# Pinning SyncE's loads to program order in a hybrid decoder layer, with the mLSTM's row of maxima on GpSimd's queue

## The chip, the cores and the metric

The kernel runs on one core of one Trainium2 chip. The metric is device time in microseconds of that core for one execution. TensorE (PE) multiplies, VectorE (DVE), ScalarE (ACT) and GpSimd (POOL) do element work, and SyncE (SP) only issues transfers. POOL and ACT issue transfers as well. Each engine takes its own instructions strictly in the order in which they stand in its queue: one that waits holds up all that stand behind it on the same engine.

## The reference, cut to what matters

One step of a one-layer decoder for 2048 prompt tokens and 8 x 4 decode tokens, model width 1024. An mLSTM head group (4 heads, keys of 64, values of 128) and a sliding-window attention group (8 heads, window 128, a learned sink per head) share one input and one output projection; a squared-ReLU MLP of width 4096 and a gated per-layer embedding follow.

```
def mlstm_chunk(state, blk):                       # 128 tokens
    b = cumsum(lf); log_d = where(causal, b_t - b_s + ig_s, -inf)
    m_t = maximum(b + m_prev, max(log_d))          # the row of maxima
    s = einsum('bhtd,bhsd->bhts', q, k) * exp(log_d - m_t)
    num = s @ v + exp(b + m_prev - m_t) * (q @ c_prev)
    den = sum(s) + exp(b + m_prev - m_t) * (q @ n_prev)
    h = num / maximum(abs(den), exp(-m_t))
...
x1 = x + rms_norm(concat(mlstm, attention) @ w_out, g_mix_post)
x2 = x1 + rms_norm(relu(rms_norm(x1, g_ffn_pre) @ w_up)**2 @ w_down, g_ffn_post)
y  = x2 + gated embedding of p through w_pgate and w_pproj
```

All of it is in float32; the kernel multiplies with a split of each operand into a high and a low part, three matmuls for one product.

## The kernel before, in words

The 2048 tokens are 16 blocks of 128 (numbered 0 to 15). The first part (0 to about 680 us) is the input projection over six chunks of 3, 3, 3, 3, 2 and 2 blocks; the mLSTM and the window attention of a chunk run as side work between the projection's matmuls. The second part goes over three groups of two chunks each: the output projection (`mo`), the MLP (`up`, `dn`) and the gate (`pg`, `pv`). In a group, two plain MLP steps are followed by 14 steps in which the up-projection is done with seven products instead of eight, from sums and differences of weight blocks (`product`); those are the product steps.

**Weights** go through a `Ring`. In the first use of a weight its raw float32 tile (`wr`, five buffers; `wb` for the product steps) is loaded on SP, ACT casts it to the high part, DVE or POOL subtracts to get the low part (`wsplit`), and POOL stores the pair to device memory (`wk<-w`). All later uses reload the pair (`w<-wk`, 512 KB, SP) into one of seven pair buffers. So the second and later chunks of a part only reload, and the third group never splits. A pair buffer comes free when PE has done the matmuls that read it: SP waits at the head of its queue for this.

**What sets the order.** The program is written as Python that emits instructions; the tile framework places every instruction on its engine's queue, and may move an instruction up or down among its neighbours unless it was marked with `here` (`tc.keep_in_program_order`), after which it keeps its turn among the others so marked. Matmuls, splits, and the stores of pairs are marked. The loads through `dma` (that is, `nc.sync.dma_start`) are not, and nor are those through `put` (`nc.gpsimd.dma_start`).

**The row of maxima.** `mbd` is a small array in device memory that holds the row of m_t for the blocks of one chunk; ACT stores it (`mbd<-Mt`, line 906). `weights(i)` (line 959) then loads it into `Wt`, the same row on all 128 partitions, 256 KB (line 961), on SP. DVE adds the causal mask (line 962), ACT takes exp (line 964), DVE multiplies by the scores (line 997, `Wt<-mS,Wt`). There are 16 such loads, one for each block, and two `Wt` buffers.

**Names that the prediction uses.** `wr<-in_w_out`, `in_w_up`, `in_w_down`: raw weights (lines 351, 363, 374); `wb<-in_w_up` (line 307): the raw tile of a product step, two for each step; `xr` (line 1460, POOL): the input block added after the output projection, used at line 1485; `y<-yd` (line 848): the mixers' output read back; `scs`, `snr`, `sso`: the decode tokens' states, loaded by POOL in group 2 of 3; `gffn`, `gpost`: the weights of the norms after the MLP and after the output projection (line 1453); `os` (line 831): sigmoid of the output gate; `hh`, `hl` (lines 231, 232): the split hidden activations; `x31t`: a transpose on PE.

Of the kernel before, what the change touches and what calls it, by code (L numbers as in the profile page):

```python
# [18 lines left out]
P = 128  # L19
# [103 lines left out]
def bc(ap, axis, n):  # L123
    v = ap.unsqueeze(axis)
    shape = list(v.shape)
    shape[axis] = n
    return v.broadcast_to(tuple(shape))
# [71 lines left out]
def hybrid_layer(ctx: ExitStack, tc: tile.TileContext, A, O):  # L199
    nc = tc.nc  # L200
    act, dve, pool = nc.scalar, nc.vector, nc.gpsimd
    pe = Flow(tc)
    swa, mls, tsp = pe.side(), pe.side(), pe.side()
    dma, put = nc.sync.dma_start, nc.gpsimd.dma_start
    here = tc.keep_in_program_order

    xp = A["x_prompt"].rearrange("b t d -> (b t) d")
    xs = A["x_sample"].rearrange("b t d -> (b t) d")
# [726 lines left out]
    def mlstm_finish(num, e_col, sig, y, n, nm):  # L935

        t = small.tile([P, 24], F32, tag="fin", name=nm + "f", bufs=2)
        den = num[:n, :, 128]
        dve.scalar_tensor_tensor(t[:n, 0:4], den, -1.0, den, ALU.mult, ALU.max)
        dve.scalar_tensor_tensor(t[:n, 4:8], e_col, 8.0, t[:n, 0:4], ALU.mult, ALU.max)  # L940
        dve.reciprocal(t[:n, 8:12], t[:n, 4:8])
        junk = jp.tile([P, MV], BF16, tag="jm", name=nm + "jm")
        for h in range(MH):
            act.activation(junk[:n], num[:n, h, 0:MV], AF.Square, scale=t[:n, 8 + h : 9 + h], accum_out=t[:n, 12 + h : 13 + h])
        dve.tensor_scalar(t[:n, 16:20], t[:n, 12:16], 1.0 / MV, EPS, ALU.mult, ALU.add)
        pool.tensor_tensor(t[:n, 20:24], t[:n, 16:20], nhalf[:n].broadcast_to((n, 4)), ALU.pow)
        dve.tensor_tensor(t[:n, 20:24], t[:n, 20:24], t[:n, 8:12], ALU.mult)
        for h in range(MH):
            c = slice(h * MV, (h + 1) * MV)
            dve.scalar_tensor_tensor(y[:n, c], num[:n, h, 0:MV], t[:n, 20 + h : 21 + h], sig[:n, c], ALU.mult, ALU.mult)  # L950

    def mlstm_chunk(r, blocks):
        nonlocal C
        qk, col = r["qk"], r["col"]
        rows = lambda h: slice((h % 2) * MK, (h % 2) * MK + MK)
        cq = lambda i, q, h: col[:, i * 16 + q * 4 + h : i * 16 + q * 4 + h + 1]
        Ws = {}

        def weights(i):
            Wt = sm.tile([P, MH, P], F32, tag="Wt", name=f"Wt{blocks[i]}")  # L960
            dma(Wt, bc(r["mbd"][:, i * P : (i + 1) * P], 0, P))
            here(dve.tensor_tensor(Wt, Wt, bc(mask, 1, MH), ALU.add))
            for h in range(MH):
                act.activation(Wt[:, h], Wt[:, h], AF.Exp, bias=cq(i, 0, h), scale=-1.0)
            Ws[i] = Wt

        todo = []

        def finish():
            if todo and len(r.get("o", ())) == len(blocks):  # L970
                i, num = todo.pop(0)
                y = sm.tile([P, 512], F32, tag="ym", name=f"ym{blocks[i]}")
                mlstm_finish(num, col[:, i * 16 + 8 : i * 16 + 12], r["o"][i], y, P, f"m{blocks[i]}")
                put(yd[blocks[i]][0], y)

        weights(0)
        yield 3.0
        for i, b in enumerate(blocks):
            c = slice(i * P, (i + 1) * P)
            v = r["v"][i]  # L980
            if i + 1 < len(blocks):
                weights(i + 1)
            pK = psum(ps_m, f"mK{b}")
            for p in range(2):
                pe.transpose(pK[:, p * P : (p + 1) * P], qk[2 + p][:, c], ident)
            kw = sm.tile([P, MH, MK], F32, tag="kw", name=f"kw{b}")
            dve.tensor_tensor(
                kw, pK[:, 0:256].rearrange("p (h d) -> p h d", h=MH), bc(col[:, i * 16 + 12 : i * 16 + 16], 2, MK), ALU.mult
            )
            yield MPACE  # L990
            pS = [psum(ps_m, f"mS{b}{e}")[:, : 2 * P].rearrange("p (h t) -> p h t", h=2) for e in range(2)]
            for h in range(MH):
                pe.matmul(pS[h % 2][:, h // 2], qk[2 + h // 2][rows(h), c], qk[h // 2][rows(h), c], start=True, stop=True)
            Wt = Ws.pop(i)
            We = Wt.rearrange("p (g e) t -> p e g t", e=2)
            for e in range(2):
                dve.tensor_tensor(We[:, e], pS[e], We[:, e], ALU.mult)
            while len(todo) > 1:
                finish()
                yield 0.5  # L1000
            num = sm.tile([P, MH, 130], F32, tag="num", name=f"num{b}")
            yield MPACE
            if C is not None:
                pX = [psum(ps_m, f"mX{b}{p}").rearrange("p (h t) -> p h t", h=2) for p in range(2)]
                for h in range(MH):
                    pe.matmul(pX[h % 2][:, h // 2, :130], qk[h // 2][rows(h), c], C[rows(h), h // 2], start=True, stop=True)
                for h in range(MH):
                    dve.tensor_scalar(num[:, h], pX[h % 2][:, h // 2, :130], cq(i, 1, h), None, ALU.mult)
                yield MPACE
            pI = [psum(ps_m, f"mI{b}{p}").rearrange("p (h t) -> p h t", h=2) for p in range(2)]  # L1010
            for h in range(MH):
                pe.matmul(pI[h // 2][:, h % 2, :130], Wt[:, h], v[:, h], start=True, stop=True)
            for p in range(2):
                n_ = num[:, 2 * p : 2 * p + 2]
                if C is None:
                    act.copy(n_, pI[p][:, :, :130])
                else:
                    dve.tensor_tensor(n_, pI[p][:, :, :130], n_, ALU.add)
            yield MPACE
            pU = psum(ps_m, f"mU{b}").rearrange("p (h t) -> p h t", h=2)  # L1020
            for h in range(MH):
                pe.matmul(pU[rows(h), h // 2, :130], kw[:, h], v[:, h], start=True, stop=True)
            Cn = sm.tile([P, 2, 130], F32, tag="C", name=f"C{b}")
            for p in range(2):
                if C is None:
                    dve.tensor_copy(Cn[:, p], pU[:, p, :130])
                else:
                    dve.scalar_tensor_tensor(
                        Cn[:, p], C[:, p], col[:, 64 + 4 * p + i : 65 + 4 * p + i], pU[:, p, :130], ALU.mult, ALU.add
                    )  # L1030
            C = Cn
            todo.append((i, num))
            finish()
            yield MPACE
        while todo:
            finish()
            yield 0.5
# [413 lines left out]
    def gain(src, nm):  # L1451
        g = gp.tile([P, D], F32, tag="g", name=nm)
        dma(g, src[0:1, :].broadcast_to((P, D)))
        return g

    gpost, gffn = gain(A["norm_mix_post"], "gpost0"), None
# [41 lines left out]
    f, yt, ut, xt = {}, {}, {}, {}  # L1498
# [126 lines left out]

    def mlp(gi, chunks, sample):
        nonlocal gffn
        gffn = gain(A["norm_ffn_post"], f"gffn{gi}")
        G = f"{gi}"
        if sample:  # L1630
            f["t"] = es2.enter_context(tc.tile_pool(name="ft", bufs=1, reuse_waits="tile")).tile(
# [154 lines left out]
        for ci in range(2):  # L1786
            if ci == 1:
                pe.drain(tsp)
                pe.drain(dec)
                es_lp.close()  # L1790
                es_t = ExitStack()
                tp = es_t.enter_context(tc.tile_pool(name="tp", bufs=1, side="right", reuse_waits="tile"))
                ring.wide = es_t.enter_context(tc.tile_pool(name="wide", bufs=WIDE, side="right", reuse_waits="tile"))
                tsp.add(sums())
            for s in range(FAST):
                if ci == 0:
                    hids.append({})
                up(s, ci, ring.take(4), hids[s])
            for s in range(FAST):
                for half in range(2):  # L1800
                    down(s, ci, half, down_weights(), hids[s])
# [23 lines left out]
    def finish(b, half, pg, pv, n, nm, last):  # L1825
        hs = slice(half * 512, half * 512 + 512)
        t = gw.tile([P, 512], F32, tag="sg", name=f"sg{nm}{half}")
        act.activation(t[:n], pg, AF.Tanh, scale=0.5)
        dve.scalar_tensor_tensor(t[:n], t[:n], 1.0, pv, ALU.add, ALU.mult)
        o = gw.tile([P, 512], F32, tag="ot", name=f"ot{nm}{half}")  # L1830
        dve.scalar_tensor_tensor(o[:n], t[:n], 0.5, f[b][:n, hs], ALU.mult, ALU.add)
        dst = y_s[:, hs] if b == "s" else y_p[b * P : (b + 1) * P, hs]
        (dma if last else put)(dst, o[:n])

    def gate_post(gi, ci, c, sample):

# [168 lines left out]
```

## Time and profile before

| what | value |
|---|---|
| time, median of 3 runs | 2611.8 us (2611.41 to 2611.95) |
| the profiled execution: time, span | 2623.78 us, 2621.7 us |
| mean granted TensorE clock | 0.989 |
| PE busy / idle | 2534.7 us (97%) / 87 us |
| DVE, ACT, POOL busy | 57%, 37%, 24% |
| transfers: mean rate, share of the 16 engines | 248 GB/s; SP's queue 53.4%, POOL's 17.3% |
| `w<-wk` on SP, 512 KB | 728 loads, 4.9 us from issue to landing (median) |
| `Wt<-mbd` on SP, 256 KB | 16 loads, 4.2 us |
| `xr` on POOL, 512 KB | 16 loads, 9.4 us |

PE is busy 97% of the span, so the time is PE's work plus what PE waits: the last is 87 us, spread over many short waits. The views of waits list what ended each wait; the timeline lists an engine's instructions with their start, their length and, in square brackets, the idle time just before and what ended it.

### The profile page before, as it was taken

The numbers are of one execution on the slowest core, as the hardware profiler recorded it, in microseconds if no ns is written. First come the engines' busy times: TensorE is split into PE (matmuls) and PEld (weight loads), VectorE is DVE, ScalarE is ACT, GpSimd is POOL, SyncE is SP. The second block draws the span as 40 slices with busy tenths as digits, with TensorE's granted clock in tenths as the row PEclk, the third lists the DMA queues.
The fourth block names the chain that finished last, engine by engine and source line by source line (L and its number), as shares of the span: only waits on it lengthen the run. The fifth ranks groups of instructions, "written<-read, shape, count | busy, mean of one in ns | idle before, by whom it ended". The sixth has DMA issues, their size and how long they took to land.

```text
span 2621.7 us, 39337 instructions
## 1 busy us (share of the span) xinstructions
PE 2534.7 (97%) x14260; PEld 2204.3 (84%) x14260; DVE 1483.0 (57%) x3162; ACT 974.3 (37%) x2167; POOL 620.3 (24%) x988
## 2 busy tenths in 40 slices
PE   7999999998999999999999999999999999999998
PEld 7787888777778888888877788999998879999986
DVE  6666656665657655656744654444446346444553
ACT  5545444544445444444523342222223134222231
POOL 5311111112433666666523200000001011000010
PEclk9999999999999999999999999999999999999999
DMA  9756656576898666666799765555556899777787
GB/s 315 273 192 201 207 181 213 194 244 227 260 343 287 254 250 253 244 254 251 271 341 318 255 201 188 188 191 188 187 187 233 295 334 359 253 255 256 256 299 235
DMA packets 220433, 651.10 MB, mean 248 GB/s; under 512 B 25397, under 2 KB 59401, under 8 KB 220224
## 3 DMA queue, kind: packets, MB, share of 16 engines
q1 hardware_dynamic: 170032, 474.02, 53.4%
q0 software_dynamic: 50160, 174.54, 17.3%
q8 instruction: 113, 1.85, 0.3%
q14 instruction: 80, 0.66, 0.1%
q10 hardware_dynamic: 48, 0.03, 0.0%
HBM read 494.34 MB, written 155.25 MB: 248 GB/s over the span
## 4 chain that ended last, share of the span: by engine, by line
PE 77%; DVE 8%; DMA 7%; issue 3%; ACT 2%; POOL 2%; SPq 0%; ACTq 0%; DVEq 0%; POOLq 0%
PE up L148 21%; PE dn L148 21%; PE mo L148 5%; PE pg L148 5%; PE v L148 3%; DMA w<-wk 3%; PE o L148 3%; DMA wk<-w 2%; PE qk L148 2%; PE qa L148 2%; PE gv L148 2%; DVE hl L232 2%; PE aT L152 1%; PE aO L148 1%; PE pv L148 1%
## 5 line engine op out<-in xcount | busy, mean ns | idle before, releaser
L148 PE MATMUL dn<-w,hh 128*128 128x512 f32 x1792 | 564.0, 396 | 6.3 <-ACT re L1654 3.8
L1759 DVE TENSOR_TENSOR f<-f,dn 128x512 f32<-128x512 f32 x420 | 286.9, 686 | 220.5 <-PE dn L148 218.4
L148 PEld LDWEIGHTS dn<-w,hh 128*128 128x128 f32 x1792 | 334.2, 189 | 84.7 <-DVE f L1759 6.8
L148 PE MATMUL dn<-w,hl 128*128 128x512 f32 x896 | 354.5, 396 | 1.6 <-DVE hl L232 1.6
L1734 DVE TENSOR_TENSOR re<-up,re 128x384 f32<-128x384 f32 (+1 forms) x294 | 151.9, 517 | 320.2 <-PE up L148 320.2
L148 PEld LDWEIGHTS dn<-w,hl 128*128 128x128 f32 x896 | 168.8, 188 | 43.5 <-DVE hl L232 5.1
L1735 ACT COPY re<-up 128x384 f32<-128x384 f32 (+1 forms) x42 | 18.8, 448 | 392.0 <-PE up L148 392.0
L1654 ACT ACTIVATE re<-re 128x384 f32<-128x384 f32 (+1 forms) x168 | 83.0, 494 | 207.5 <-DVE re L1734 203.9
L232 DVE TENSOR_TENSOR hl<-re,hh 128x384 fp32r<-128x384 f32 (+1 forms) x192 | 137.6, 717 | 16.8 <-ACT hh L231 15.7
L282 POOL DMA_DIRECT2D wk<-w x242 | 134.1, 556 | 34.4 <-DVE w L255 25.2
L254 ACT CAST w<-wr 128x512 fp32r<-128x512 f32 (+2 forms) x152 | 88.9, 597 | 95.9 <-PE up L148 32.3
L254 ACT CAST w<-wb 128x512 fp32r<-128x512 f32 x98 | 60.6, 620 | 168.4 <-PE dn L148 114.6
L255 POOL TENSOR_TENSOR w<-wr,w 128x512 fp32r<-128x512 f32 (+2 forms) x76 | 100.2, 1319 | 80.5 <-ACT w L254 79.5
L255 POOL TENSOR_TENSOR w<-wb,w 128x512 fp32r<-128x512 f32 x70 | 92.3, 1319 | 110.3 <-ACT w L254 109.8
L1460 POOL DMA_DIRECT2D x<-x1d x16 | 8.7, 545 | 463.5 <-PE up L148 449.4
L1655 ACT ACTIVATE re<-re 128x384 f32<-128x384 f32 (+1 forms) x192 | 94.9, 494 | 5.9
L231 ACT CAST hh<-re 128x384 fp32r<-128x384 f32 (+1 forms) x192 | 92.6, 482 | 8.3
L1067 ACT ACTIVATE s<-s,swt 128x257 f32<-128x257 f32 (+1 forms) x128 | 63.3, 496 | 65.8 <-DVE swt L1064 65.8
L1061 DVE CUSTOM_DVE_ANT_0 s<-aS,cst,sink 128x256 f32<-128x256 f32 (+1 forms) x128 | 57.1, 472 | 52.0 <-PE aS L148 51.6
L148 PE MATMUL up<-t2h,w 128*128 128x384 f32 (+1 forms) x336 | 85.1, 320 | 0.0
L148 PE MATMUL up<-t0h,w 128*128 128x384 f32 (+1 forms) x336 | 85.1, 320 | 0.0
L148 PE MATMUL up<-t1h,w 128*128 128x384 f32 (+1 forms) x336 | 85.1, 320 | 0.0
(1526 smaller groups left out, 6415.7 us busy)
## 6 DMA issues: line engine op xcount, KB each, us to landing
w<-wk SPq DMA_DIRECT2D x728, 512.0 KB, 4.9
wk<-w POOLq DMA_DIRECT2D x238, 512.0 KB, 7.2
wr<-in_w_down_dram SPq DMA_DIRECT2D x64, 256.0 KB, 8.2
wb<-in_w_up_dram SPq DMA_DIRECT2D x28, 512.0 KB, 6.9
w<-wk SPq DMA_DIRECT2D x20, 528.0 KB, 3.9
x<-in_x_prompt_dram SPq DMA_DIRECT2D x16, 512.0 KB, 4.4
y<-yd SPq DMA_DIRECT2D x32, 256.0 KB, 7.0
xr<-in_x_prompt_dram POOLq DMA_DIRECT2D x16, 512.0 KB, 9.4
```

The source lines that it names most:

```text
L148: ins = self.pe.matmul(out, lhsT, rhs, start=start, stop=stop)
L231: act.copy(hi, src)
L232: dve.tensor_tensor(lo, src, hi.bitcast(F32), ALU.subtract)
L254: act.copy(hi, src)
L255: ins = (eng or weng()).tensor_tensor(lo, src, hi.bitcast(F32), ALU.subtract)
L282: here(put(self.kept[key], t.bitcast(U32)))
L1061: dve.tensor_tensor_reduce(s_[:, s, lo : 2 * P], pS[:, s, lo:], bias[:, j, lo:], 1.0 if s == 0 else 0.0625, sink[:, h : h + 1], ALU.add, A ...
L1067: act.activation(e_, e_, AF.Exp, bias=nm[:, s : s + 1], accum_out=sm[:, s : s + 1])
L1654: act.activation(t, src, AF.Relu)
L1655: act.square(t, t)
L1734: add = lambda out, a, b: dve.tensor_tensor(out, a, b, ALU.add)
L1759: dve.tensor_tensor(out(i), out(i), ps, ALU.add)
```

## The change

`dma` becomes a function that issues the load on SP as before and marks it with `here`: all loads of SP's queue keep the turn in which the program emits them. The only transfers of SP that stay unmarked are the last two output stores. The load of `Wt` goes by `put`, that is by POOL's queue, and is not marked. The load of `gffn` moves from the start of `mlp` to its second chunk, after the drain of the side work.

```
-    dma, put = nc.sync.dma_start, nc.gpsimd.dma_start
+    put = nc.gpsimd.dma_start
     here = tc.keep_in_program_order
+
+    def dma(out, src):
+
+        here(nc.sync.dma_start(out, src))
...
         def weights(i):
             Wt = sm.tile([P, MH, P], F32, tag="Wt", name=f"Wt{blocks[i]}")
-            dma(Wt, bc(r["mbd"][:, i * P : (i + 1) * P], 0, P))
+            put(Wt, bc(r["mbd"][:, i * P : (i + 1) * P], 0, P))
...
     def mlp(gi, chunks, sample):
         nonlocal gffn
-        gffn = gain(A["norm_ffn_post"], f"gffn{gi}")
...
             if ci == 1:
                 pe.drain(tsp)
+                gffn = gain(A["norm_ffn_post"], f"gffn{gi}")
                 pe.drain(dec)
...
-        (dma if last else put)(dst, o[:n])
+        (nc.sync.dma_start if last else put)(dst, o[:n])
```

In the changed kernel PE has the same 13662 matmuls in the same order. SP has 16 transfers fewer and 103 others in another place, POOL 16 more and 16 others in another place; 35 instructions of ACT and 62 of DVE stand a few places away. Three places matter.

SP at the start of the second chunk, before the change. `wr<-in_w_out` is a raw weight of the output projection, which is used some 560 us later; `w<-wk` are the second chunk's first reloads; `Wt_1414` is the row of maxima of block 2:

```order
L351 DMA wr_7677<-in_w_out_dram 128x512
L351 DMA wr_7683<-in_w_out_dram 128x512
L351 DMA wr_7752<-in_w_out_dram 128x512
L351 DMA wr_7759<-in_w_out_dram 128x512
L289 DMA w_1497<-wk_193 128x1056
L289 DMA w_1500<-wk_200 128x1056
L289 DMA w_1503<-wk_208 128x1056
L961 DMA Wt_1414<-mbd_626 128x4x128
L363 DMA wr_7799<-in_w_out_dram 64x512
L289 DMA w_1505<-wk_216 128x1056
```

After the change the reloads follow the projection's last raw weight, and the first rows of `w_out` stand where the first group begins, the third behind the six `y` loads of the second chunk:

```order
L209 DMA wr_1474<-in_w_in_dram 128x512
L209 DMA w_1497<-wk_193 128x1056
L209 DMA w_1500<-wk_200 128x1056
L209 DMA w_1503<-wk_208 128x1056
L209 DMA w_1505<-wk_216 128x1056
...
L209 DMA wr_7677<-in_w_out_dram 128x512
L209 DMA wr_7683<-in_w_out_dram 128x512
L209 DMA y_7721<-yd_108 128x512
...
L209 DMA wr_7752<-in_w_out_dram 128x512
```

So four raw tiles and a half left the early place, and `Wt_1414` left SP. Likewise, in the first group, four raw tiles of `w_up` that stood ahead of the sixteen reloads of `w_out` for the second chunk, and one that stood among them, stand behind them now; the first `wb` tiles stand behind the last sixteen reloads of `w_down`'s plain steps instead of behind the eleventh.

ACT in the last product step of the first group, before. `w_13207`, `w_13214`, `w_13221`, `w_13228` are the casts of the four `w_down` weights of that step, which PE needs as soon as the step's `up` matmuls end; `re` and `hh` are the hidden activations of its four parts:

```order
L254 CAST w_13207<-wr_13209 128x512
L254 CAST w_13214<-wr_13216 128x512
L1654 ACTIVATE re_13033<-re_13033 128x384
L1655 ACTIVATE re_13033<-re_13033 128x384
L231 CAST hh_13080<-re_13033 128x384
L254 CAST w_13221<-wr_13223 128x512
L254 CAST w_13228<-wr_13230 128x512
```

And after:

```order
L236 CAST hh_13171<-re_13034 128x384
L259 CAST w_13207<-wr_13209 128x512
L1658 ACTIVATE re_13032<-re_13032 128x384
L259 CAST w_13214<-wr_13216 128x512
L1659 ACTIVATE re_13032<-re_13032 128x384
L259 CAST w_13221<-wr_13223 128x512
L236 CAST hh_13198<-re_13032 128x384
L259 CAST w_13228<-wr_13230 128x512
```

The four casts went behind three of the four parts' activations; the other 13 product steps keep their order on ACT.

POOL in the second group's output projection, before. `xr` are the three residual blocks of the group's first chunk:

```order
L1460 DMA xr_14626<-in_x_prompt_dram 128x1024
L1263 MEMSET scs 128x16
L1272 DMA scs<-in_state_mlstm_c_dram 64x4x128
L1460 DMA xr_14638<-in_x_prompt_dram 128x1024
L1272 DMA scs<-in_state_mlstm_c_dram 64x4x128 x2
L1460 DMA xr_14650<-in_x_prompt_dram 128x1024
...
L1298 DMA sso<-zsd 32x512
```

And after:

```order
L1277 DMA scs<-in_state_mlstm_c_dram 64x4x128 x4
L1279 DMA snr<-in_state_mlstm_n_dram 4x64 x4
L1303 DMA sso<-zsd 32x512
L1465 DMA xr_14626<-in_x_prompt_dram 128x1024
L1465 DMA xr_14638<-in_x_prompt_dram 128x1024
L1465 DMA xr_14650<-in_x_prompt_dram 128x1024
```

The three residual loads went behind all the decode states' loads.

## The prediction

> **What bounds the kernel now.** I read the page's busy shares first, then the waits of PE, then the waits of SP.
>
> ```profile
> span 2621.7 us, 39337 instructions
> PE 2534.7 (97%) x14260; PEld 2204.3 (84%) x14260; DVE 1483.0 (57%) x3162; ACT 974.3 (37%) x2167; POOL 620.3 (24%) x988
> ```
>
> PE is busy 2534.7 of 2621.7 us. Its work and its order stay the same, so all that the change can give or take lies in PE's 87 us of idle time, or adds to it. The waits of PE:
>
> ```profile
> PE mo L148 <- DMA w<-wk: 5.5, 3, 2.8
> PE qk L148 <- DMA w<-wk: 4.5, 3, 3.9
> PE x31t L152 <- ACT os L831: 3.0, 1, 3.0
> ```
>
> The columns are the sum, the number of waits and the longest. Only some ten of the 87 us wait for a reload directly. The waits of SP show what can hold the reloads up:
>
> ```profile
> SPq L961 <- DMA mbd<-Mt: 33.1, 6, 7.0
> ```
>
> Six times SP stood at its queue's head with a `Wt` load whose source had not been stored yet. That hurts only where the reloads behind it were due.
>
> **The change part by part.** A minus is a gain.
>
> *Wt off SP, sixth chunk.* SP's and PE's timelines:
>
> ```profile
> 597.95 3.50 SPq L289 DMA_DIRECT2D w<-wk  x4
> 608.20 0.92 SPq L961 DMA_DIRECT2D Wt<-mbd  x2
> 609.22 1.99 SPq L289 DMA_DIRECT2D w<-wk  x4
> 614.84 0.58 PE L148 MATMUL qk<-x5h,w 128*128 128x256 f32 x1 [3.91 <-DMA w<-wk]
> ```
>
> From 601.5 to 608.2 SP waited for `mbd`; right behind the two `Wt` loads four reloads went out within 2 us, so their buffers were free before. PE then idled 3.91 us for one of them. Without the `Wt` load at the head they leave up to 6.7 us sooner, which covers the wait: -3.9 (bounds -3.9 and -1, if the last of the four buffers was free only shortly before). On POOL the `Wt` load stands behind copies that it makes later than 608, so nothing on POOL waits for `mbd`, and DVE's masking of these two is some 50 us away.
>
> *Wt off SP and w_out's raw weights off the early place, second chunk.*
>
> ```profile
> 113.69 0.33 SPq L351 DMA_DIRECT2D wr<-in_w_out_dram  x1
> 118.36 1.20 SPq L961 DMA_DIRECT2D Wt<-mbd  x1
> 126.97 0.69 DVE L962 TENSOR_TENSOR Wt<-Wt,cst 128x512 f32<-128x512 f32 x1 [2.67 <-DMA Wt<-mbd]
> 132.43 1.12 PE L152 MATMUL x31t<-ident,x 128*128 128x128 f32 x4 [2.99 <-ACT os L831]
> DMA to landing us min/median/max: 3.2/4.2/8.6
> ```
>
> The `Wt` load of block 2 left at 118.36 behind raw weights that waited for raw buffers until 113.69, landed 8.6 us later (the longest of the 16, the last row), and DVE idled 2.67 us for it; ACT's work for PE's transpose is behind that. On POOL it stands right after the last stores of this stretch. If it leaves at about 116 and lands in 4.2 to 8.6 us, DVE no longer waits. I take -2.0; bounds -3.0 (PE's whole wait) and 0.
>
> The Trainium skill ("DMA: Bandwidth & Descriptors", section "Specifications") puts the first byte of a transfer from GpSimd's queue about 0.4 us later than from SyncE's (1 against 0.6). By that the gain is 2.0 too. The rows of this case are harsher: 512 KB takes 9.4 us on POOL (`xr`, below), far above SP's reloads; 5 us more would leave nothing of it. That is the bound of 0.
>
> *w_up's raws behind the reloads, first group.*
>
> ```profile
> 701.00 14.38 SPq L374 DMA_DIRECT2D wr<-in_w_up_dram  x4
> 715.48 9.64 SPq L289 DMA_DIRECT2D w<-wk  x5
> 733.15 1.51 SPq L289 DMA_DIRECT2D w<-wk  x3
> 741.54 0.73 PE L148 MATMUL mo<-w,yt01h 128*128 128x512 f32 x2 [1.99 <-DMA w<-wk]
> ```
>
> Four `w_up` raws held SP for 14.38 us, since each waits for a raw buffer, with the first reload behind them; a later reload left at 733.15 and PE idled 1.99 us. Now the reloads go first: -2.0 (bounds -2.0 and 0, as the 733.15 load had to wait for its own buffer too). The `w_up` raws then come behind the sixteenth reload, about 750, and PE's `up` begins near 769; a raw of that size lands in 3 to 5 us and its split takes 2: covered.
>
> *Casts of the last product step.* ACT's casts and PE's first `dn`:
>
> ```profile
> 1264.51 0.62 ACT L254 CAST w<-wr 128x512 fp32r<-128x512 f32 x1
> 1270.48 0.62 ACT L254 CAST w<-wr 128x512 fp32r<-128x512 f32 x1 [1.42 <-PE up L148]
> 1276.34 0.51 ACT L231 CAST hh<-re 128x384 fp32r<-128x384 f32 x1
> 1276.55 0.62 PE L148 MATMUL dn<-w,hh 128*128 128x512 f32 x2
> ```
>
> The first and the fourth cast were done by 1271.1, five us before PE needs them. Now the first follows the third part's `hh`, which ends at 1276.85. With 0.62 for each cast, three activations of about 0.52 between them and 0.7 to 1.3 for the subtraction, the first pair is ready at about 1278.3 and the fourth at 1281.6 to 1282.2. PE wants the first at 1276.55 and, at three matmuls of 0.23 us for each pair, the fourth at 1278.65. So PE waits 1.7 (first pair only) to 3.5: +2.4.
>
> *xr behind the decode loads, second group.*
>
> ```profile
> 1407.52 0.56 POOL L1460 DMA_DIRECT2D xr<-in_x_prompt_dram  x1
> 1424.72 0.53 POOL L1298 DMA_DIRECT2D sso<-zsd  x1 [0.44 <-DMA scs<-in_state_mlstm_c_dram]
> 1429.86 0.75 DVE L1485 SCALAR_TENSOR_TENSOR f<-f,ms,xr 128x512 f32<-128x512 f32 x1
> 1433.76 1.86 PE L148 MATMUL dpd<-dec,cb 8*128 8x4 f32 x8
> xr<-in_x_prompt_dram POOLq DMA_DIRECT2D x16, 512.0 KB, 9.4
> ```
>
> Before, the third `xr` left at 1407.52 and DVE used the first at 1429.86. Now they follow `sso`, which left at 1424.72 and perhaps some us sooner without three large loads ahead of it: 1419 to 1425 plus 9.4 is 1428 to 1434. DVE may stand there for up to 4.5 us, with the copies for PE's `dpd` (1433.76) behind it. +1.0, bounds 0 and +4.5.
>
> *w_out's first rows late, first group.*
>
> ```profile
> 663.42 3.83 SPq L848 DMA_DIRECT2D y<-yd  x6
> 666.93 1.13 ACT L254 CAST w<-wr 128x512 fp32r<-128x512 f32 x2
> 670.27 0.76 DVE L997 TENSOR_TENSOR Wt<-mS,Wt 128x256 f32<-128x256 f32 x2 [0.82 <-PE mS L148]
> wr<-in_w_out_dram SPq DMA_DIRECT2D x8, 256.0 KB, 4.5
> ```
>
> These raws lay ready since 114; now they leave at about 663.4, where the `y` loads left, and land 4.5 us later, at 668 to 668.5, when ACT's casts stood at 666.93. A subtraction on DVE follows the second cast and stands ahead of `Wt<-mS`, which the mLSTM's next matmuls on PE read. The third raw comes behind six `y` loads and holds ACT again. +1.0, bounds 0 and +4.
>
> *First wb later.*
>
> ```profile
> 822.19 2.70 SPq L307 DMA_DIRECT2D wb<-in_w_up_dram  x2
> 825.62 6.96 SPq L289 DMA_DIRECT2D w<-wk  x5
> 834.11 0.69 DVE L255 TENSOR_TENSOR w<-wb,w 128x512 fp32r<-128x512 f32 x1 [2.72 <-ACT w L254]
> 845.28 0.34 PE L148 MATMUL up<-ut00h,w 128*128 128x384 f32 x1
> wb<-in_w_up_dram SPq DMA_DIRECT2D x28, 512.0 KB, 6.9
> ```
>
> The two `wb` of the first product step leave after the fifth of those reloads, at about 832.6 instead of 822.19, and land 6.9 us later, at 839.5. Cast and subtraction end near 841.5; PE needs the pair at 845.28. But DVE's subtraction stands ahead of its `dn` sums, which wait with it for about 2.5 us. +0.6, bounds 0 and +3.
>
> *The rest, at nothing.* In the 14 product steps `wb` of a step now comes behind all four `w_down` raws of the step before. Both are loaded a step of 32 us ahead, which covers a shift of 9 us. PE's waits there name DVE, and no load:
>
> ```profile
> PE dn L148 <- DVE f L1759: 2.5, 10, 0.3
> ```
>
> Taken as 0, with bounds of -2.5 and +2. The second chunk's `x` loads come later by nine raws; they would land near 60 and ACT reads the first here:
>
> ```profile
> 73.61 1.06 ACT L516 ACTIVATE x3j<-x 128x1024 bf16<-128x1024 f32 x1
> ```
>
> The twelve other `Wt` loads and `gffn` (last read behind the product steps) have tens of us.
>
> **Sum.** Gains 3.9 + 2.0 + 2.0 = 7.9; losses 2.4 + 1.0 + 1.0 + 0.6 = 5.0. Net -2.9 us on a profiled time of 2623.78 (span 2621.7 and 2.1 around it), so 2620.9 there. The runs' median of 2611.8 lies 12.0 below the profiled time, and the same step puts it at 2608.9. About 0.2%, 5.2 us, is what can be told from no change.
>
> **The rivals.**
>
> *More is gained than the terms say.* SP's head of queue also shifts transfers that I could not follow: 1.25 MB of `w_out` raws leave the crowded first 130 us, where PE idles 20 us. If half the bounds above come true together (-3.9, -3.0, -2.0, -2.5 against +2.4 and nothing else) it is -9.0, and with 2 us more of the early idle time -11: 2600.8 to 2602.8. For it: the early waits of PE are chains through loads. Against: those chains name ACT and DVE, and they keep their order.
>
> *The in-order engines turn the late loads into a loss.* One mechanism: a load that was early is now just in time, and ACT and DVE stand before it with PE's next operands behind them. It strikes at 668 (w_out), at 1430 (`xr`) and at 839 (`wb`). With the upper bounds, 4 + 4.5 + 3 + the casts' 3.5 = 15.0, less the gains of 7.9, it is +7.1: 2618.9. It decides from the point where raws take as long as `w_down`'s in the product steps, some 8 us, instead of 4.5. For it: the `y` loads beside them take 7. Against: each place has some us of slack in the rows above.
>
> *The removed waits come back elsewhere.* PE gets the reload earlier, and meets the next late operand a few matmuls on (DVE's or ACT's): gains of 7.9 shrink to about 4, and with 5.0 of losses it is +1.0: 2612.8.
>
> **How the numbers follow.** Forecast 0.42: 2608.9, with 2604 to 2613 as its own range. More gained 0.24: about 2602. Waits come back 0.17: 2612.8. Loss by in-order engines 0.17: 2619. Faster by over 5.2 us: all of the second case and a third of the forecast's, 0.38. Slower by over 5.2: most of the last case, 0.03 from the third: 0.18. Same: 0.44. The range for 8 in 10 runs from 2598 to 2618.
>
> **What would show it right or wrong.** Right: PE's wait before `qk` at 614.84 is gone and SP has no wait for `mbd`; DVE does not idle before `Wt` near 127; `mo` near 741 does not wait; PE waits about 2 us for DVE or POOL `w` at the first `dn` near 1277. Wrong: DVE idle before `f<-f,ms,xr` near 1430 or before `w<-wr` near 668 of more than 2 us, with PE idle behind it; or the whole first 130 us shifted by more than 3 us, which I have not priced.

## The result, and the profile after

| | before | after |
|---|---|---|
| time, median | 2611.88 us (2611.41 to 2612.75) | 2634.43 us (2632.68 to 2635.98) |
| ratio after / before | | 1.0086, 95% interval 1.0068 to 1.0103 |
| profiled execution: time, span | 2623.78, 2621.7 us | 2633.93, 2632.1 us |

The change makes the kernel 22.5 us slower. The forecast was 2608.9 us, a small gain, and its range ended at 2618.

The page's busy shares of the changed kernel:

```profile
span 2632.1 us, 39327 instructions
PE 2535.8 (96%) x14260; PEld 2203.5 (84%) x14260; DVE 1488.2 (57%) x3162; ACT 969.2 (37%) x2167; POOL 632.1 (24%) x1004
```

PE does the same work in the same order, so the loss is idle time, or matmuls that run slower. The waits of PE that matter, after (sum, count, longest):

```profile
PE pg L148 <- DMA w<-wk: 9.9, 3, 8.1
PE v L148 <- ACT u L772: 8.1, 2, 7.1
PE dn L148 <- ACT re L1658: 6.3, 2, 4.2
PE mo L148 <- DMA w<-wk: 5.4, 6, 1.8
PE xt20t L152 <- DVE xt00l L237: 2.3, 1, 2.3
PE dpd L148 <- DVE dec L1215: 2.0, 1, 2.0
PE yt0t L152 <- DVE Wt L1002: 1.4, 1, 1.4
PE up L148 <- ACT re L1739: 1.3, 1, 1.3
PE dn L148 <- POOL w L260: 1.0, 1, 1.0
```

The wait of `qk` (3.9) and that of `x31t` (3.0) that the prediction quoted are gone, and SP has no wait for `mbd` any more. The `mo` reloads cost what they cost before (5.4 against 5.5; a second execution of the kernel before, e1 below, has 8.0). Two rows that the prediction did not have stand out. The first is at the very end. PE and then SP, after:

```profile
2594.95 1.09 PE L148 MATMUL pg0s<-w,sx 128*64 128x512 f32 x4
2604.17 1.19 PE L148 MATMUL pg<-w,xt21h 128*128 128x512 f32 x2 [8.12 <-DMA w<-wk]
...
2560.24 24.56 SPq L209 DMA_DIRECT2D w<-wk  x12
2595.82 1.74 SPq L1838 DMA_DIRECT2D out_dram<-ot  x2
2599.90 0.33 SPq L1838 DMA_DIRECT2D out_dram<-ots  x1
2600.32 13.95 SPq L209 DMA_DIRECT2D w<-wk  x10
```

SP's last reload ahead of the stores has left by 2584.80. Then three output stores stand at SP's head and wait for their results, the first until 2595.82 and the third until 2599.90; the last ten reloads of weights, now behind them, leave from 2600.32, and PE stands 8.12 us. (The output stores of SP that the change leaves unmarked are six, three for each half of the columns, and not two as said above; these are the first three.) Before, six of these ten reloads had left ahead of the stores, in a row of 27:

```profile
2543.25 53.23 SPq L289 DMA_DIRECT2D w<-wk  x27
2596.52 1.58 SPq L1833 DMA_DIRECT2D out_dram<-ot  x2
2598.20 2.01 SPq L289 DMA_DIRECT2D w<-wk  x2
```

The second is in the second group, in the last plain MLP steps of its second chunk, just ahead of the product steps. PE and ACT, after:

```profile
1551.96 0.40 PE L148 MATMUL dn<-w,hl 128*128 128x512 f32 x1
1556.58 1.22 PE L148 MATMUL dn<-w,hh 128*128 128x512 f32 x2 [4.22 <-ACT re L1658]
1558.03 1.05 PE L148 MATMUL dn<-w,hh 128*128 128x512 f32 x2
1558.88 0.63 PE L148 MATMUL dn<-w,hl 128*128 128x512 f32 x1
...
1537.09 0.84 ACT L1704 CAST t0h<-ts 128x768 fp32r<-128x768 f32 x1 [4.10 <-DVE ts L1691]
1539.82 0.84 ACT L1704 CAST t1h<-ts 128x768 fp32r<-128x768 f32 x1 [1.90 <-DVE ts L1695]
1543.30 0.83 ACT L1704 CAST t2h<-ts 128x768 fp32r<-128x768 f32 x1 [2.64 <-DVE ts L1699]
1544.15 0.49 ACT L1658 ACTIVATE re<-up 128x384 f32<-128x384 f32 x1
1556.04 0.48 ACT L1658 ACTIVATE re<-up 128x384 f32<-128x384 f32 x1
```

ACT stands 8.6 us for sums that DVE makes for the coming product steps (`t0h` to `t2h`), with `re`, which reads the up-projection's sums out of PE's accumulation buffers, behind them. The kernel has three of these buffers (`ps_mm`) for `up` and `dn` alike. PE's next `dn` had been ready at 1552.36 and waits for the buffer that the fourth `re` empties from 1556.04 to 1556.52; it goes on at 1556.58, before the cast behind that `re` begins (1557.11), so it is the buffer that it lacks and not the activation.

### The profile page after: what moved, and what is told of

It is laid out like the page before. It is cut to its first block, busy times and chain, and to the rows that moved or that the text cites. A ratio compares the mean times of both kernels' runs of the same rounds, so it can differ in the third digit from the quotient of the medians.

```text
span 2632.1 us, 39327 instructions
## 1 busy us (share of the span) xinstructions
PE 2535.8 (96%) x14260; PEld 2203.5 (84%) x14260; DVE 1488.2 (57%) x3162; ACT 969.2 (37%) x2167; POOL 632.1 (24%) x1004
## 5 line engine op out<-in xcount | busy, mean ns | idle before, releaser
L237 DVE TENSOR_TENSOR hl<-re,hh 128x384 fp32r<-128x384 f32 (+1 forms) x192 | 119.1, 620 | 21.4 <-ACT hh L236 20.0
L260 DVE TENSOR_TENSOR w<-wr,w 128x512 fp32r<-128x512 f32 (+2 forms) x76 | 79.1, 1047 | 38.7 <-ACT w L259 32.1
```

Of the source, the lines that this page charges most:

```text
L237: dve.tensor_tensor(lo, src, hi.bitcast(F32), ALU.subtract)
L260: ins = (eng or weng()).tensor_tensor(lo, src, hi.bitcast(F32), ALU.subtract)
```

## The experiments

The kernel before was timed beside them on each chip, with medians of 2609.1 to 2612.0, and the ratios are to it. Where two traces are compared, the matmuls were matched one by one (PE's 14260 instructions stand in the same order in all of these kernels).

**e1: the kernel before, profiled again.** No edit.

> The kernel before, unchanged, for a second trace. Its first trace took 2623.8 us, its timed runs 2611.9. If the first trace was taken in an execution that waited more than usual, this one is near 2612 and lacks some of the waits that the prediction wanted to remove (3.9 us before qk at 614.8, 3.0 before x31t, 2.0 before mo at 741.5). If profiling itself costs 12 us, it is near 2624 again with the same waits.

2607.59 us, span 2605.5. The trace from which the prediction argued (2623.78) was an unusually slow execution, slower than every timed run of that kernel. Its mean granted clock is lower, 0.989 against 0.994. Matched, 5 of its extra 16 us lie between 700 and 750 us, about two `mo` waits of 3.7 and 2.0 us; this execution has one of 2.4 us there and three under 1 us. The `qk` and `x31t` waits are in both.

**e2: the change, with the last six stores on GpSimd's queue.**

```diff
-        (nc.sync.dma_start if last else put)(dst, o[:n])
+        put(dst, o[:n])
```

> The change, with the six last output stores on GpSimd's queue instead of SyncE's. Theory: pinning the loads let the three unmarked stores of the last gate's first half pass ten reloads, and PE waited 8.1 us for one of these. Then PE's wait before pg near 2604 is gone and the time is 8 to 11 us under the change's 2634.4: 2624 to 2626. Rival (the reloads were late for lack of bandwidth, or the stores then make the last transfer late): 2632 or more.

2627.54 us, ratio 1.006 (1.0045 to 1.0075): 6.9 us faster than the change, and 1.5 us above the range that was expected. The stall at `pg` is gone (10.8 us earlier there), but the end pays for it:

```profile
2613.84 1.08 PE L148 MATMUL pg1s<-w,sx 128*64 128x512 f32 x4
2619.04 0.51 POOL L1838 DMA_DIRECT2D out_dram<-ots  x1 [2.12 <-DVE ots L1836]
```

From the last matmul's start to the end of the span (2626.3) it is 12.5 us, against 7.7 in the change (2624.42 to 2632.1). The stores ahead of the reloads are a cause, worth some 10 us.

**e3 and e4: loads marked in the projection and the first group alone, and in the first two groups.**

```diff
-        here(nc.sync.dma_start(out, src))
+        ins = nc.sync.dma_start(out, src)
+        if loadpin:
+            here(ins)
...
+        loadpin = gi == 0            # e4: gi <= 1; at the start of each group
...
-        (nc.sync.dma_start if last else put)(dst, o[:n])
+        (dma if last else put)(dst, o[:n])
```

> Loads of SyncE marked in the projection and the first group only; Wt on GpSimd and gffn as in the change. ACT's casts of the last product step, the second group's ACT, DVE and POOL orders and the last stores are back where the kernel before has them. Theory (three late places hold the loss, the early part gains): the trace keeps the lead of some 18 us at the first group's last product step and gives none back: 22 to 27 us under the change, 2608 to 2613, and under the kernel before if its 18 us were real in timed runs too. Rival (the loss is spread or lies in the early part): over 2620.

> Loads marked through the second group, not in the third: the order at the last product step of the first group and in the second group is the change's, the last stores and the third group are as before. Theory: it loses the 16 us of the gate and of the second group but not the 8 to 11 us of the last stores: 2623 to 2626, like the stores on GpSimd.

e3: 2609.72, ratio 0.9992 (0.998 to 1.0004), the kernel before within what can be told. e4: 2618.35, ratio 1.0031 (1.002 to 1.0042), where 2623 to 2626 was expected; more of the loss than expected is left for the third group. Between the two matched traces e4 loses 7.7 us from 1500 to 1600, of which 4.39 in one step, at the `dn` above. Another 2.9 us are lost between 1450 and 1500, about a wait of PE of 2.5 us before `ut100t` near 1490, which is 1.5 us in e3. So the net loss lies behind the first group, part of it in the second and part in the third.

**e5: the Wt loads on GpSimd's queue, alone**, in the kernel before.

```diff
-            dma(Wt, bc(r["mbd"][:, i * P : (i + 1) * P], 0, P))
+            put(Wt, bc(r["mbd"][:, i * P : (i + 1) * P], 0, P))
```

> The kernel before with one edit: the 16 Wt loads go by POOL's queue; nothing is marked, gffn stays. Theory (the change is a sum of separate bills, and the Wt move is its gain): PE's wait for a reload before qk near 609 goes, and with it some 4.5 to 6.5 us, as the matched matmuls of the run with the first group marked gained there against the kernel before; the second chunk's x loads stay early, so PE does not wait 3.8 us for v near 76. About 2605 where the kernel before gives 2610.6 (-5). Rival (the gain at 609 is taken back by the next late operand): within 2 us of the kernel before.

2605.54, ratio 0.998 (0.9971 to 0.9989): the theory. PE's rows of an ordinary execution of the kernel before, ahead of the two places:

```profile
609.25 0.58 PE L148 MATMUL qk<-x5h,w 128*128 128x256 f32 x1 [4.33 <-DMA w<-wk]
130.45 0.66 PE L152 MATMUL x31t<-ident,x 128*128 128x128 f32 x4 [2.92 <-ACT os L831]
```

and of e5, where `qk` has no wait at all:

```profile
128.55 0.65 PE L152 MATMUL x31t<-ident,x 128*128 128x128 f32 x4 [0.97 <-ACT os L831]
```

**e6: besides, the product steps' loads marked** (first group, second product step to the last but one; `gffn` moved as in the change, which alone changes no other instruction's place).

```diff
+    loadpin = False
...
+            loadpin = gi == 0 and FAST + 1 <= s < STEPS - 1
             up_both(s, X, hid)
```

> As the Wt move alone, and the loads of the first group's product steps marked, from the second step to the one before the last; ACT and DVE keep the order of the Wt move alone. Theory: wb of a step behind the w_down raws of the step before gains about 0.4 us in each of some ten steps, as the matched matmuls show between 850 and 1250 us (-4 to -5): about 2601. Rival (that gain belongs to the clock or to the reordered casts, not to the loads' turn): as the Wt move alone, within 1 us.

2599.93, ratio 0.9959 (0.9946 to 0.9971): the theory, and the fastest version here, faster than both kernels. Why a later `wb` gains is in DVE's and POOL's rows. e5, around one step, and the groups of its DVE from 865 to 1245 us (count | busy, mean ns):

```profile
939.43 2.62 DVE L232 TENSOR_TENSOR hl<-re,hh 128x384 fp32r<-128x384 f32 x1
...
945.50 0.55 DVE L232 TENSOR_TENSOR hl<-re,hh 128x384 fp32r<-128x384 f32 x1
...
939.07 1.31 POOL L314 TENSOR_TENSOR wb<-wb 128x512 f32<-128x512 f32 x1
940.33 1.29 POOL L313 TENSOR_TENSOR wb<-wb,wb 128x512 f32<-128x512 f32 x1
...
L232 DVE TENSOR_TENSOR hl<-re,hh 128x384 fp32r<-128x384 f32 x48 | 56.9, 1185 | 1.3 <-ACT hh L231 1.3
```

and e6:

```profile
948.30 1.28 POOL L322 TENSOR_TENSOR wb<-wb,wb 128x512 f32<-128x512 f32 x1 [9.23 <-DMA wb<-in_w_up_dram]
...
L241 DVE TENSOR_TENSOR hl<-re,hh 128x384 fp32r<-128x384 f32 x48 | 40.3, 840 | 6.3 <-ACT hh L240 6.3
```

In e5 DVE's subtraction `hl`, 0.55 us where it is undisturbed, takes 2.62 while GpSimd sums `wb`. In e6 `wb` lands later, GpSimd's sum of two starts at 948.30 instead of 940.33, behind `hl`, whose mean falls from 1185 to 840 ns. PE gets some 0.4 us in nine of the steps, 4.8 us in all from 850 to 1250: its waits for DVE's sum `f` between 865 and 1245 us fall from 2.3 us (eight waits) to 0.6 us (one). ACT, DVE and GpSimd keep e5's order and only some loads of SP have another turn, so the late load gains because it moves GpSimd's work away from DVE's.

**e7 and e8: the change's marks up to the product steps.** The first group's loads are marked until its last product step, and all later loads are free.

```diff
             hid = {}
+            if s == STEPS - 1:
+                loadpin = False
```

In e8, besides, the `x` loads of the projection go by `nc.sync.dma_start`, unmarked.

> The change with loads marked only from the start to the last product step of the first group but one; the last product step, the gate of the first group and all behind have their loads free, the last stores as before. Theory: against the run with the whole first group marked (2609.7) this leaves out the reordered casts of the last product step and the gate, which cost 6 to 7 us between 1250 and 1450: 2603. Rival (those 7 us are the clock's, not the order's): 2609 to 2610, as that run.

> As the run marked up to the product steps, but the x loads of the projection's chunks are not marked, so the second chunk's go out ahead of the raw weights again. Theory: PE's wait of some 7 us for v near 76 shrinks to what it was (3.5 us), 4 us less than that run: 2599. Rival (the raws that now come behind x are late in their place): equal to that run, or slower.

e7: 2603.94, ratio 0.9969 (0.9957 to 0.9981). e8: 2600.59, ratio 0.996 (0.9948 to 0.9973). Both as the theory had them, though the gain of e8 over e7, 3.4 us, is no more than the intervals allow. PE, e7 and then e8:

```profile
79.61 1.22 PE L148 MATMUL v<-w,x0h 128*128 128x512 f32 x2 [7.23 <-ACT u L776]
```

```profile
77.34 1.22 PE L148 MATMUL v<-w,x0h 128*128 128x512 f32 x2 [4.54 <-ACT u L776]
```

e3 against e7 is the last product step and the gate of the first group: 6 us by the ratios, 6 to 7 by the matched traces (1250 to 1350 us). PE's waits in the first part of the gate, e7 and then the change:

```profile
1282.90 0.66 PE L152 MATMUL xt10t<-ident,f 128*128 128x128 f32 x4 [0.30 <-DVE xt00l L241]
1284.95 0.66 PE L152 MATMUL xt20t<-ident,f 128*128 128x128 f32 x4 [0.80 <-DVE xt00l L241]
```

```profile
1259.10 0.50 PE L148 MATMUL dn<-w,hh 128*128 128x512 f32 x1 [0.74 <-ACT w L259]
1260.60 0.50 PE L148 MATMUL dn<-w,hh 128*128 128x512 f32 x1 [1.00 <-POOL w L260]
1288.94 1.12 PE L152 MATMUL xt20t<-ident,f 128*128 128x128 f32 x4 [2.29 <-DVE xt00l L237]
1287.06 0.62 ACT L259 CAST w<-wr 128x512 fp32r<-128x512 f32 x1 [1.43 <-DMA wr<-in_w_pgate_dram]
1287.58 0.58 ACT L236 CAST xt00h<-xt10t 128x512 fp32r<-128x512 f32 x1
```

ACT waits for a raw gate weight with the cast of `xt` behind it. Between e7 and e3 both ACT's order and the turn of the raw gate weights on SP differ there, and no run tells the two apart.

**e9: two groups marked (e4), but the reloads free.** **e10: two groups marked, but the gain loads (`gffn`, `gpost`) free.**

```diff
-                dma(t.bitcast(U32), self.kept[key])                  # e9
+                nc.sync.dma_start(t.bitcast(U32), self.kept[key])
...
-        dma(g, src[0:1, :].broadcast_to((P, D)))                     # e10
+        nc.sync.dma_start(g, src[0:1, :].broadcast_to((P, D)))
```

> As the run with the first two groups marked, but the reloads w<-wk are not marked; the raws, wb, x, y, p and gain loads of these groups are. SyncE's queue then stands as in that run but for four places; the order of ACT, DVE and GpSimd is that of the run with the first group alone marked: in the second group's first product step re stands ahead of the casts t0h to t2h again, and xr goes out ahead of the decode states. Theory (the 9 us of the second group come from the order of ACT and DVE, not from SyncE's queue): PE's wait of some 4 us before dn near 1557 is gone, 2609 to 2610 against 2618.4. Rival (they come from loads that SyncE now issues later: gpost, y, p): 2617 to 2618.

> As the run with the first two groups marked, but the gain loads (gffn, gpost) are not marked; ACT and DVE keep that run's order, and on GpSimd's queue xr goes out ahead of the decode states again. Theory: only the 1 to 2 us of the late xr in the second group are gained, and PE's wait before dn near 1557 stays: 2616.5 to 2617.5. Rival (the late xr shifts the second group's casts and is the cause of all 9): 2609 to 2610.

e9: 2608.14, ratio 0.9993 (0.9982 to 1.0004), as the theory had it: SP's queue as in e4 but for four places, ACT, DVE and GpSimd as in e3, and the second group's loss is gone, the 2.9 us ahead of 1500 too. It is the order of ACT and DVE that costs (that of GpSimd does not: e10 below has e9's but for one store, and PE's 4.2 us before `dn` are there), and marking the reloads brings that order about, although their own turn on SP hardly changes. ACT at that place in e9, `re` ahead of the casts:

```profile
1535.47 0.49 ACT L1662 ACTIVATE re<-up 128x384 f32<-128x384 f32 x1 [2.61 <-PE up L148]
1535.86 0.83 ACT L1708 CAST t0h<-ts 128x768 fp32r<-128x768 f32 x1
```

e10: 2624.88, ratio 1.0055 (1.0043 to 1.0067): neither answer. It was to be 1 to 2 us faster than e4 and was 6.5 slower. Its trace, matched with e4's, differs by 2 us.

**e12 and e13: e4 and e10 again, on one chip.**

> The kernel with the first two groups marked again, beside the next one on one chip. Theory (the 6 us by which the run with free gain loads was slower come from the chip and its clock, since the two traces, matched matmul by matmul, differ by 2 us): both within 3 us of each other. Rival (the gain loads' place really costs 6 us): this one at 2618 and the next at 2624 to 2625.

> The kernel with the first two groups marked and the gain loads free, again, on the same chip as the one before. Theory: within 3 us of it. Rival: 6 us slower than it, as before.

2621.55 (ratio 1.0032, 1.002 to 1.0044) and 2621.74 (1.0043, 1.0031 to 1.0055): the same within the intervals. So the order of those loads is not worth the 6.5 us of e10; they came with that set of runs, on another chip, and what made them stays open. A difference of some 6 us between runs on different chips, even as ratios, is therefore not read here without the matched traces. One thing of e10 holds: with `xr` ahead of the decode states again (13 to 16 us sooner than in e4), PE waits for `dec` as long as in e4, 1.9 to 2.0 us.

**e11: the change with the second group free and the last stores marked.**

```diff
+        loadpin = gi != 1
...
-        (nc.sync.dma_start if last else put)(dst, o[:n])
+        (dma if last else put)(dst, o[:n])
```

> The change with the second group's loads unmarked and the last stores as before; the first and the third group are marked. Theory: the whole loss of the change lies in the last stores (8 us and what the slower matmuls behind the stall add) and in the second group (9 us); without these two it is as the run with the first group alone marked, 2609 to 2610. Rival (the third group's marked loads cost something beyond the stores): 2612 or more.

2620.4, ratio 1.0037 (1.0023 to 1.0052), where 2609 to 2610 was expected. A premise of the expectation was wrong. Marked, the stores do not stand "as before": they keep the program's turn, which is ahead of the last ten reloads. PE in e11:

```profile
2592.43 1.19 PE L148 MATMUL pg<-w,xt21h 128*128 128x512 f32 x2 [8.20 <-DMA w<-wk]
```

So the stall does not come from stores that were left unmarked. The program gives them that turn; before, the framework had moved the unmarked reloads ahead of them, and the marks take this freedom away. Between 2550 us and the end the matched traces of e3 and e11 differ by 10.8 us, and by nothing else of that size; ACT keeps e3's order there but for one instruction, DVE but for two, and GpSimd keeps it wholly.

**The sum**, by the ratios, each step against the one above (0.001 is 2.6 us, and an interval is some 3 us to each side). The steps to e3 and to the change go from one chip to another; the matched traces give 6 to 7 and 11.8 us for them, and 10.8 for the stores:

| what is added | from, to | us |
|---|---|---|
| Wt by GpSimd's queue | 1, 0.9980 | -5.2 |
| product steps' loads marked | 0.9980, 0.9959 | -5.5 |
| the other loads up to the product steps, without x | 0.9959, 0.9960 | +0.3 |
| the x loads | 0.9960, 0.9969 | +2.4 |
| last product step and gate, first group | 0.9969, 0.9992 | +6.0 |
| second group | 0.9992, 1.0031 | +10.2 |
| third group (the same step from e3 to e11: +11.7) | 1.0031, 1.0086 | +14.4 |

## Why the prediction was wrong, point by point

- **Wt off SP, sixth chunk (-3.9) and second chunk (-2.0)**: right. In e5 the matched matmuls gain 4.5 us at `qk` (6.6 between 600 and 650) and 1.9 at `x31t`. The bound of "5 us more" for the load on POOL did not come: `Wt` lands in 5.9 us there (median; the longest is 11.9), against 4.2 (8.6).
- **w_up's raws behind the reloads (-2.0)**: wrong. The wait near 741 was larger in the trace from which the prediction argued; in the change four waits for reloads between 714 and 738 us sum to 3.7 us (1.2 and 1.8 at 716 and 719), against 4.1 in e1.
- **Casts of the last product step (+2.4)**: right in place and size: 0.74 and 1.00 us of waiting, 2.3 us in the matched traces from e7 to e3. What followed was missed: the loads and ACT's casts stand in another order through the gate as well, which made it +6.0.
- **xr behind the decode loads (+1.0)**: the wrong cause. `xr` left at 1407 to 1410 and not at 1419 to 1425, since the small decode loads no longer stood behind three large ones, and the wait for `dec` is there with `xr` early as well (e10). In e1 PE waits 1.8 us for a reload just ahead of that place, in the change 2.0 us for `dec` and for no reload, and the matched traces lose nothing there: a wait that came back elsewhere, as the third rival had it.
- **w_out's first rows (+1.0), first wb (+0.6)**: right within their bounds: PE waits 1.4 us at `yt0t` and 1.3 at `up` near 838.
- **"The rest, at nothing"**: the 14 product steps, "Taken as 0, with bounds of -2.5 and +2", were worth -5.5 (4.8 in the matched traces), outside the bounds. The prediction read PE's waits there as naming "DVE, and no load"; but the loads' turn set when GpSimd worked beside DVE, and these waits are what went. That the second chunk's `x` loads "would land near 60" missed the raw weight that now stood behind them: ACT idled 3.52 us for it (row below), and PE's wait before `v` near 76 grew from 4.1 (e1) to 7.1. PE was 2.7 us late at 90 us; at 130 us it was level with e1 again, the `x31t` wait being gone, so the whole first 130 us did not shift, as the prediction's sign had it. The two errors have opposite signs. ACT, after:

```profile
66.89 0.62 ACT L259 CAST w<-wr 128x512 fp32r<-128x512 f32 x1 [3.52 <-DMA wr<-in_w_in_dram]
```

- **Not in the sum at all**: the last stores (+10.8 in the matched traces) and the second group (+10.2). These two are the error, and the step that failed: the prediction priced transfers that moved on SP and POOL, and put at nothing, without a reason, the 35 instructions of ACT and 62 of DVE that its own look at the change had counted as "a few places away", and the ten reloads that now stand behind unmarked stores. In the runs each of the two is an in-order queue whose head waits: ACT for DVE's sums (4.22 us of PE, 7.7 us with what is around it), SP for the results to be stored (8.12 us of PE). It also priced waits alone, and the slower matmuls behind a long wait (last section) add to both.

The rival that went to the right side, in-order engines behind late loads, named three places (668, 1430, 839), of which the first and the last hold some 3 us of the loss. Its mechanism, an in-order queue whose head waits with something due behind it, is the one that decided, but on SP at 2596 behind stores and on ACT at 1537 behind casts.

## What to carry to other kernels

When a change freezes an order, price every instruction that stands elsewhere afterwards on every engine, and look first at those that were *not* frozen and at the last transfers, where nothing behind can hide a wait. A queue whose head waits for a result must have nothing behind it that is due sooner: read, for each store on a load queue, when its source is ready and which loads follow. Freeze only where the trace shows a gain: here one move (the `Wt` loads off SP) and one frozen loop (the product steps) gave 10.7 us together, and marking everything else cost three times that.

## What the runs showed of the hardware

**A stall costs more than its length.** The windows of the change around its two stalls (busy us, count, then granted clock PEclk):

```profile
core 0: us, PE busy (x) PEld busy (x) DVE busy (x) ACT busy (x) POOL busy (x), PEclk, DMA share, GB/s
1555.00:1560.00 5.00, 3.42 (x8) 2.75 (x9) 4.96 (x7) 3.23 (x6) 0.00 (x0) 0.50 0.16 29
2605.00:2610.00 5.00, 4.99 (x13) 3.28 (x13) 0.00 (x0) 0.00 (x0) 0.00 (x0) 0.57 1.03 419
2610.00:2615.00 5.00, 5.00 (x23) 3.77 (x22) 0.00 (x0) 0.00 (x0) 0.00 (x0) 1.00 0.90 294
```

After 4.2 and 8.1 us of waiting the clock granted to PE is 0.50 and 0.57, behind the second with 13 matmuls in 5 us instead of 23; the matmuls follow each other in 0.43 us (two from 1558.03 to 1558.88) instead of 0.23, for some 4 to 5 us. By the matched traces that adds 1.7 and 2.5 us to the two stalls. The Trainium skill ("TensorE: Matmul & The Clock Gate", section "Part 1: The HAM clock gate") says that an idle window of about 3.4 us drops the array to half rate, and that about as long of sustained work brings it back, counted in windows that run free of the kernel. The 0.43 us agree with its 426.7 ns; its 215.7 ns at full rate is a little less than the 0.23 here. That the windows run free would make waits of 2 to 3 us cost differently from one execution to the next. The two traces of the kernel before show such a difference once: behind its wait of 2.99 us before `x31t` the first was granted 0.50 from 132 to 137 us, with 24 matmuls in these 5 us, and e1, behind a wait of 2.92 us, 1.00 from 130 to 135 us, with 46; matched, that is some 2.7 us. Whether it is what spreads the times of the kernel before, from 2604.3 to 2621.0 us, is not shown.

**GpSimd's sums hold DVE's subtractions up.** The `hl` row above: a subtraction with both inputs in on-chip memory took 2.62 us beside two GpSimd sums that ended at 941.62, and would have taken 0.55. The Trainium skill ("SBUF — State Buffer", section "Who interferes with whom") says that such a DVE instruction and a GpSimd instruction that reads the same memory share a port, and calls that an exclusive lock; the times agree, and the port itself is in no row.
